# Rotary embedding on one core: the order of the loads and stores behind the fifth tile

## Chip, core and metric

The kernel runs on one NeuronCore of a Trainium2 chip. The metric is the device time of one launch in microseconds (us). Every time below is from six runs of the kernel before, or from one profiled execution of it.

## What is computed

The input x is a float32 array of 16 batches, 512 positions and 1024 numbers, 33.55 MB. The 1024 numbers are 16 heads of 64. In each head the first 32 numbers (x1) and the last 32 (x2) are turned against each other by the position's cosines and sines:

```python
x = x.reshape(batch, seq, num_heads, head_dim)
x1, x2 = (x[..., :half_dim].copy(), x[..., half_dim:].copy())
cos = cos[None, :, None, :].copy()
sin = sin[None, :, None, :].copy()
rotated = np.concatenate([x1 * cos - x2 * sin, x1 * sin + x2 * cos], axis=-1)
```

The output has the same size as x, so each number is read once, goes through a few operations, and is written once.

## The kernel before

**Tiles.** Two batches make a tile of 128 partitions: 64 partitions for each batch, and 8 positions (rows, k = 0 to 7) of 1024 numbers in every partition. That is 32 KB in a partition and 4.19 MB in a tile. There are NT = 8 tiles, numbered 0 to 7. Below, L3 is the load of tile 3 and S3 the store of tile 3.

**Buffers.** The pool `xp` has BUFS = 5 buffers of one tile each. The result is written over the input in the same buffer, and the store leaves from it. So tile 5 goes into the buffer of tile 0, tile 6 into that of tile 1, tile 7 into that of tile 2, and the load of tile n has to wait until the store of tile n - 5 has landed.

**Who does what.** For each row, GpSimd multiplies the swapped halves by the signed sines into a buffer `b` (line 155; seven rows of eight), VectorE multiplies the row by the cosines into a PSUM tile `ps` (line 156), and the two are added: by VectorE (line 145) for five rows, and for the rows 1, 4 and 6 by two TensorE matmuls with an identity (line 164), after which ScalarE copies the sum into the tile (line 167). In row 6 VectorE makes both products (lines 156 and 158). There are six buffers `b` and three of `ps`, so that GpSimd may run ahead of VectorE by some rows.

**The order of the transfers.** All DMAs are issued from one engine, SyncE (SP), in the order of the program: `load` is line 72, `store` line 76. The program runs under a manual schedule, so this order is the one written here. SP carries out one instruction after the other. Where a DMA has to wait, for its tile's last row or for a buffer to come free, all that is behind it on SP waits too.

Ahead of the loop stand tile 0 in four parts (lines 78 and 84), the two tables (lines 81 and 82) and the loads of tiles 1 to 4 (line 86). In the loop (lines 147 to 180), tile t is computed, then stored (line 173; the last tile in two halves, line 177), and behind the store of tile t, from t = 1 on, the load of tile t + 4 is issued (lines 179 and 180) as long as there is one. From the first store on, SP's order is therefore

```
S0 S1 L5 S2 L6 S3 L7 S4 S5 S6 S7(first half) S7(second half)
```

Of the kernel before, what the change touches and what calls it, by code (L numbers as in the profile page):

```python
# [13 lines left out]
BUFS = 5  # L14
# [12 lines left out]
def kernel(  # L27
# [21 lines left out]
    NT = batch // NB  # L49
# [18 lines left out]
    def load(t, lo=0, hi=KK):  # L68
        if tiles[t] is None:
            tiles[t] = xp.tile([P, F], FP32, name="xt")  # L70
        s = slice(lo * dim, hi * dim)
        nc.sync.dma_start(out=tiles[t][:, s], in_=x_v[t][:, s])  # L72

    def store(t, lo=0, hi=KK):
        s = slice(lo * dim, hi * dim)
        nc.sync.dma_start(out=out_v[t][:, s], in_=tiles[t][:, s])
# [36 lines left out]
    def cos_b(k):  # L113
        c = cos_t[:, k * half : (k + 1) * half]
        return bass.AP(tensor=c.tensor, offset=c.offset, ap=[c.ap[0], [0, 2 * nh], [1, half]])

    def over_heads(s):
        return bass.AP(tensor=s.tensor, offset=s.offset, ap=[s.ap[0], [0, nh], [1, hd]])

    def swapped(r, n):  # L120
        return bass.AP(
            tensor=r.tensor, offset=r.offset + half, ap=[r.ap[0], [hd, n], [-half, 2], [1, half]]
        )

    def swapped_signed(i):

        s = sns_t[:, i * hd : (i + 1) * hd]
        return bass.AP(
            tensor=s.tensor, offset=s.offset + half, ap=[s.ap[0], [0, nh], [-half, 2], [1, half]]
        )  # L130

    def pairs(r):
        return r.rearrange("p (a j) -> p a j", j=half)
# [4 lines left out]
    def halves(r):  # L138
        return r.rearrange("p (h a j) -> p h a j", a=2, j=half)
# [3 lines left out]
    def add():  # L143
        r, ps, b = pending.pop(0)
        nc.vector.tensor_tensor(out=r, in0=ps, in1=b, op=ALU.add)  # L145

    for t in range(NT):
        xt = tiles[t]
        for k in range(KK):
            r = xt[:, k * dim : (k + 1) * dim]  # L150
            ps = pr.tile([P, dim], FP32, name="ps")
            if k not in DVE_B:
                b = bp.tile([P, dim], FP32, name="b")
                sk = sns[:, k].rearrange("p a j -> p (a j)")
                nc.gpsimd.tensor_tensor(out=halves(b), in0=swapped(r, nh), in1=over_heads(sk), op=ALU.mult)  # L155
            nc.vector.tensor_tensor(out=pairs(ps), in0=pairs(r), in1=cos_b(k), op=ALU.mult)  # L156
            if k in DVE_B:
                nc.vector.tensor_tensor(  # L158
                    out=halves(r), in0=halves(r), in1=swapped_signed(DVE_B.index(k)), op=ALU.mult
                )  # L160
            if k in PE_ROWS:
                for c in range(0, dim, BANK):
                    rhs = swapped(r[:, c : c + BANK], BANK // hd) if k in DVE_B else b[:, c : c + BANK]
                    nc.tensor.matmul(  # L164
                        out=ps[:, c : c + BANK], lhsT=ident, rhs=rhs, start=False, stop=True, skip_group_check=True
                    )
                nc.scalar.copy(out=r, in_=ps)  # L167
            else:
                pending.append((r, ps, b))
            while len(pending) > (1 if k + 1 < KK else 0):  # L170
                add()
        if t < NT - 1:
            store(t)
        else:
            lo = 0
            for hi in LAST_OUT:
                store(t, lo, hi)
                lo = hi
        if t >= 1 and t + BUFS - 1 < NT:
            load(t + BUFS - 1)  # L180


# [33 lines left out]
```

## Time and profile before

| what | value |
|---|---|
| median of 6 runs | 164.62 us (164.43 to 165.4) |
| the profiled execution, its own time | 164.45 us |
| its span, first to last instruction | 162.5 us |
| VectorE busy | 132.3 us, 81% of the span |
| GpSimd busy | 130.2 us, 80% |
| TensorE matmuls busy | 82.7 us, 51% |
| ScalarE busy | 25.6 us, 16% |
| DMA packets | 3042, 67.26 MB, mean 414 GB/s |
| whole-tile loads, median from issue to landing | 29.7 us (7 of them) |
| whole-tile stores, median from issue to landing | 29.1 us (7 of them) |
| halves of the last store | 14.2 us (2 of them) |

The span is what the profiler saw between the first and the last instruction; the execution's own time has 1.95 us more around it. "Issue to landing" runs from the instruction on SP to the moment when the last of the 16 DMA engines has reported its share. It holds the transfer itself and the time that it stood in the queue behind earlier transfers. In the slices of the span (40 equal pieces of 4.06 us) a digit is a share in tenths, and 9 means 90% or more. In the views of SP a line such as `63.26 0.34 SPq L72` is an instruction that starts at 63.26 us and takes 0.34 us to issue. In the list of waits, the three numbers are the total in us, how many waits, and the longest.

### The profile page before, as it was taken

To read this page: it belongs to the slowest core of one execution; us is meant where nothing else is said; L and a number is where in the kernel's file an instruction comes from. 1 tells how busy PE (TensorE), PEld (TensorE's weight loads), DVE (VectorE), ACT (ScalarE), POOL (GpSimd) and SP (SyncE) were. 2 spreads that over 40 slices of the span, in tenths; PEclk is the share of its full clock that TensorE was granted. 3 is DMA by queue.
4 is the path that set the end of the run, shared out by engine and by line. 5 is a ranking of instruction groups with operands and counts; after the bars stand their busy time and mean duration, and the time that the engine had idled before them with its cause. 6 is when DMAs were issued, how large, how long until landed. Compare 5 with 4: busy or idle time off the path is not lost.

```text
span 162.5 us, 602 instructions
## 1 busy us (share of the span) xinstructions
PE 82.7 (51%) x106; PEld 25.7 (16%) x106; DVE 132.3 (81%) x118; ACT 25.6 (16%) x25; POOL 130.2 (80%) x62
## 2 busy tenths in 40 slices
PE   6207282644728362745663785289429833872000
PEld 1102021112202120211121212112102210220000
DVE  1197638999999999999999999999999999992000
ACT  0000511220220222022202210211220222022000
POOL 1099999999999999999999999999997999200000
PEclk9955555597895879695675558555955585557655
DMA  5999999998999999999999999999999999999991
GB/s 177 383 421 470 435 460 395 444 460 387 452 452 371 435 443 411 454 427 419 427 435 411 460 421 403 460 427 419 468 403 411 468 411 443 452 395 419 427 431 60
DMA packets 3042, 67.26 MB, mean 414 GB/s; under 512 B 352, under 2 KB 480, under 8 KB 480
## 3 DMA queue, kind: packets, MB, share of 16 engines
q1 hardware_dynamic: 3040, 67.24, 97.2%
q14 instruction: 2, 0.02, 0.0%
HBM read 33.69 MB, written 33.55 MB: 414 GB/s over the span
## 4 chain that ended last, share of the span: by engine, by line
DVE 55%; PE 12%; issue 10%; POOL 7%; ACT 4%; DMA 3%; SPq 0%; DVEq 0%; POOLq 0%
DVE ps L156 32%; DVE xt L145 17%; PE ps L164 12%; POOL b L155 7%; DVE xt L158 6%; ACT xt L167 4%; DMA b<-in_sin_dram 3%; PE tab L104 0%; PE tab L105 0%; DVE sns L107 0%; SPq L72 0%; DVE sns L108 0%; DVEq L156 0%; POOLq L155 0%
## 5 line engine op out<-in xcount | busy, mean ns | idle before, releaser
L155 POOL TENSOR_TENSOR b<-xt,sns 128x1024 f32<-128x1024 f32 x56 | 129.5, 2346 | 8.2 <-DVE sns L108 7.1
L156 DVE TENSOR_TENSOR ps<-xt,tab 128x1024 f32<-128x1024 f32 x64 | 76.7, 1226 | 6.8 <-ACT xt L167 5.8
L164 PE MATMUL ps<-b,ident 128*128 128x512 f32 x64 | 52.5, 968 | 49.2 <-DVE ps L156 40.5
L145 DVE TENSOR_TENSOR xt<-ps,b 128x1024 f32<-128x1024 f32 x40 | 48.1, 1218 | 0.9 <-POOL b L155 0.9
L167 ACT COPY xt<-ps 128x1024 f32<-128x1024 f32 x24 | 24.3, 1012 | 105.9 <-PE ps L164 95.0
L164 PE MATMUL ps<-xt,ident 128*128 128x512 f32 x32 | 26.4, 972 | 11.8 <-DVE xt L158 8.1
L164 PEld LDWEIGHTS ps<-b,ident 128*128 128x128 f32 x64 | 15.9, 273 | 83.1 <-issue 43.7
L164 PEld LDWEIGHTS ps<-xt,ident 128*128 128x128 f32 x32 | 8.4, 290 | 31.3 <-DVE xt L158 18.9
L158 DVE TENSOR_TENSOR xt<-xt,tab 128x1024 f32<-128x1024 f32 x8 | 9.8, 1221 | 0.3
L107 DVE TENSOR_SCALAR sns<-tab 128x256 f32<-128x256 f32 x1 | 0.4, 425 | 5.9 <-PE tab L105 5.9
L167 ACT ACT_TABLE_LOAD x1 | 1.3, 1283 | 16.9 <-PE ps L164 16.9
L95 PE MATMUL ps<-zero 128*128 128x512 bf16 x6 | 2.7, 627 | 1.2 <-DVE zero L89 1.2
L104 PE MATMUL tab<-b,spread 64*128 64x256 f32 x2 | 0.7, 414 | 2.5 <-DMA b<-in_sin_dram 2.5
L95 PEld LDWEIGHTS <-zero 128*128 128x128 bf16 x6 | 0.7, 135 | 2.3 <-DVE zero L89 1.2
L89 DVE MEMSET zero<- 128x256 uint32 x1 | 0.3, 272 | 0.9 <-PEq L197 0.9
L104 PEld LDWEIGHTS tab<-b,spread 64*128 64x128 f32 x2 | 0.3, 184 | 3.4 <-issue 3.4
L105 PE MATMUL tab<-b,spread 64*128 64x256 f32 x2 | 0.6, 376 | 0.0
L103 DVE COPY spread<-ident 64x64 f32<-64x64 f32 x2 | 0.3, 184 | 0.2 <-POOL ident masks.py:199 0.2
masks.py:197 POOL MEMSET ident<- 128x128 f32 x1 | 0.2, 204 | 0.3 <-POOLq L197 0.3
L108 DVE COPY sns<-tab 128x256 f32<-128x256 f32 x1 | 0.4, 415 | 0.0
L105 PEld LDWEIGHTS tab<-b,spread 64*128 64x128 f32 x2 | 0.4, 184 | 0.1
masks.py:199 POOL TENSOR_SCALAR_AFFINE_SELECT ident<-ident 128x128 f32<-128x128 f32 x1 | 0.3, 292 | 0.1
(5 smaller groups left out, 0.6 us busy)
## 6 DMA issues: line engine op xcount, KB each, us to landing
xt<-in_x_dram SPq DMA_DIRECT2D x7, 4096.0 KB, 29.7
out_dram<-xt SPq DMA_DIRECT2D x7, 4096.0 KB, 29.1
xt<-in_x_dram SPq DMA_DIRECT2D x4, 1024.0 KB, 7.6
out_dram<-xt SPq DMA_DIRECT2D x2, 2048.0 KB, 14.2
b<-in_sin_dram SPq DMA_DIRECT2D x1, 64.0 KB, 5.1
b<-in_cos_dram SPq DMA_DIRECT2D x1, 64.0 KB, 4.9
```

The costliest lines, as they stand in the source:

```text
L89: nc.vector.memset(zero, 0.0)
L95: nc.tensor.matmul(out=ps[:, c : c + BANK], lhsT=zero[:, :P], rhs=zero, start=True, stop=True)
L104: nc.tensor.matmul(out=sin_t, lhsT=spread, rhs=sin_sb, start=True, stop=True)
L105: nc.tensor.matmul(out=cos_t, lhsT=spread, rhs=cos_sb, start=True, stop=True)
L107: nc.vector.tensor_scalar_mul(out=sns[:, :, 0, :], in0=sin_k, scalar1=-1.0)
L108: nc.vector.tensor_copy(out=sns[:, :, 1, :], in_=sin_k)
L145: nc.vector.tensor_tensor(out=r, in0=ps, in1=b, op=ALU.add)
L155: nc.gpsimd.tensor_tensor(out=halves(b), in0=swapped(r, nh), in1=over_heads(sk), op=ALU.mult)
L156: nc.vector.tensor_tensor(out=pairs(ps), in0=pairs(r), in1=cos_b(k), op=ALU.mult)
L158: nc.vector.tensor_tensor(out=halves(r), in0=halves(r), in1=swapped_signed(DVE_B.index(k)), op=ALU.mult)
L164: nc.tensor.matmul(out=ps[:, c : c + BANK], lhsT=ident, rhs=rhs, start=False, stop=True, skip_group_check=True)
L167: nc.scalar.copy(out=r, in_=ps)
```

## The change

In the loop the rule for the later loads is replaced. Loads 5, 6 and 7 are now all issued in one place, behind the store of tile NT - BUFS - 1 = 2, in place of one behind each of the stores of tiles 1, 2 and 3.

```diff
@@ -176,8 +176,9 @@
             for hi in LAST_OUT:
                 store(t, lo, hi)
                 lo = hi
-        if t >= 1 and t + BUFS - 1 < NT:
-            load(t + BUFS - 1)
+        if t + 1 == NT - BUFS:
+            for n in range(BUFS, NT):
+                load(n)
```

From the first store on, SP's order becomes

```
S0 S1 S2 L5 L6 L7 S3 S4 S5 S6 S7(first half) S7(second half)
```

Nothing else differs: the instructions of the four compute engines, their order, the sizes of the transfers and the buffers are the same. Each of the three loads still waits for the store that was in its buffer (S0, S1 and S2).

## The prediction

> **What bounds the kernel now.** I read the slices of the span first, with the DMA queues below them.
>
> ```profile
> POOL 1099999999999999999999999999997999200000
> ...
> DMA  5999999998999999999999999999999999999991
> ...
> q1 hardware_dynamic: 3040, 67.24, 97.2%
> ...
> HBM read 33.69 MB, written 33.55 MB: 414 GB/s over the span
> ```
>
> The DMA row stands at nine tenths or more from the second slice to the last but one, and goes on when GpSimd and every other engine are empty. One queue, q1, holds all transfers and fills 97.2% of the 16 engines' span. The chain of waits says something else: it follows compute (VectorE 55% of it), down to the copy on ScalarE at 147.42 us that releases the last store. That chain leaves out the queue. The last store's own view tells it:
>
> ```profile
> L76 SPq DMA_DIRECT2D out_dram<-xt x1: 333/333/333, 148.5 to 148.5; - x1
> ...
> DMA to landing us min/median/max: 12.9/12.9/12.9
> ```
>
> This half store of 2 MB is issued at 148.5 and lands 12.9 us later. By the trace's landing records the store ahead of it lands at 156.53 and it lands at 161.37, so 4.84 us is its own time and about 8 us is standing in line. Compute could end 8 us later and nothing would change. The bound is the line of transfers.
>
> Now the line itself. Each transfer lands 16 times, once for each DMA engine; the last of the 16 counts. Calling load and store of tile n Ln and Sn, those records give: L1 23.73, L2 33.44, L3 43.15, L4 53.49, S0 63.18, S1 72.88, L5 83.13, S2 92.82, L6 102.97, S3 112.72, L7 122.61, S4 132.30, S5 141.97, S6 151.67, and S7 in two halves 156.53 and 161.37. (The issue plus the time to landing gives the same to 0.1 us: 148.5 + 12.9 = 161.4.) The steps between them:
>
> - load behind load: 9.71, 9.71
> - store behind store: 9.70, 9.67, 9.70; two halves 4.86 and 4.84
> - store behind load: S0 9.69, S2 9.69, S3 9.75, S4 9.69
> - a load that a store follows: L4 10.34, L5 10.25, L6 10.15, L7 9.89
>
> So a load with a store behind it ends late, by 0.63, 0.54, 0.44 and 0.18 us over 9.71. The packet records say where in the load: a 32 KB packet takes 1.213 us nearly everywhere, but from 79.6 to 81.3 us, at the end of L5, some fifteen take 1.24 to 1.56 us, likewise at 97.0 to 101.2 (L6), 118.7 to 120.4 (L7) and, longest, up to 1.94 us, at 49.3 to 51.5 (L4). The starts of L5, L6 and L7, where a load follows a store, show none to speak of. The turn from load to store costs; the turn back does not. The first engine to land loses nothing over these rounds (S1 71.98 to S4 129.76 us, 57.8 for six transfers), but the last sets the end, and the gap between first and last grows from 0.9 us at S1 to 2.5 at S4 and stays there to the end.
>
> **The change, part by part.** The same 20 DMAs of the same sizes go out and no compute instruction moves on its engine; only SP's order differs. Before, behind S1: L5 S2 L6 S3 L7 S4 S5 S6 S7. After: S2 L5 L6 L7 S3 S4 S5 S6 S7. Loads with a store behind them: four before (L4, L5, L6, L7), two after (L4, L7).
>
> *The line.* L4, S0 and S1 are as before: S1 at 72.88. Behind it: S2 9.69, L5 and L6 at 9.71 each, L7 at 9.71 plus one turn, S3 to S6 at 9.69 each, S7 9.70. Without the turn: 72.88 + 9.69 + 29.13 + 38.76 + 9.70 = 160.16. One turn is the unknown. Rows of the same kind give 0.18 (L7), 0.44 (L6), 0.54 (L5) and 0.63 (L4). They fall as the engines drift apart (first to last 0.9 us ahead of L5, 1.65 ahead of L6, 2.2 ahead of L7), so they look like the price of all engines turning together. In the new order the spread ahead of L7 should still be S1's 0.9, hence I take L5's 0.54: the last store lands at 160.70 against 161.37, **0.67 us earlier**. The ends: a turn at nothing saves 1.21; one that costs as much as the three it replaces (1.16) saves 0.05, the 0.05 being S3's slow step.
>
> *Does the line stay full?* SP's timeline of before:
>
> ```profile
> 47.20 0.34 SPq L76 DMA_DIRECT2D out_dram<-xt  x1
> 63.26 0.34 SPq L72 DMA_DIRECT2D xt<-in_x_dram  x1
> 63.70 0.90 SPq L76 DMA_DIRECT2D out_dram<-xt  x1
> 72.96 0.34 SPq L72 DMA_DIRECT2D xt<-in_x_dram  x1
> 81.12 0.33 SPq L76 DMA_DIRECT2D out_dram<-xt  x1
> 92.89 0.34 SPq L72 DMA_DIRECT2D xt<-in_x_dram  x1
> ```
>
> and from the queue's waits (total, number, longest):
>
> ```profile
> SPq L72 <- DMA out_dram<-xt: 35.3, 3, 15.6
> ```
>
> Issues take 0.34 us each, and three loads wait 35.3 us in all for the store that empties their buffer. SP stands still meanwhile, and the next store behind it too. New times: S2 waits for tile 2's last copy as it does now and is out by 64.6. L5 needs S0 landed (63.18), so it goes at about 64.7. L6 needs S1: 72.9. L7 needs S2, landing at 72.88 + 9.69 = 82.57. So SP waits some 8 and 9 us, two waits in place of three. Behind the L7 wait stands only S3, ready at 81.1, now issued at 83.0, 1.9 us later. The queue at each moment: S1 runs to 72.9 with S2 and L5 behind; S2 to 82.6 with L5 and L6; L5 to 92.3 with L6, L7, S3; S3's turn comes at about 112. No order is nearer than 8 us to being late. Cost nothing.
>
> *Does compute get its tiles in time?* L5 lands at about 92.3 instead of 83.1, 9.2 us later; L6 at 102.0, 1 us earlier; L7 at 112.2, 10.4 us earlier. GpSimd (line 155) is first at each tile; its starts by the trace are 89.24 (tile 5), 105.42, and for the last tile
>
> ```profile
> 122.77 16.23 POOL L155 TENSOR_TENSOR b<-xt,sns 128x1024 f32<-128x1024 f32 x7 [1.15 <-DMA xt<-in_x_dram]
> ```
>
> There it waits 1.15 us for L7. That wait goes, and one of about 3.1 us at tile 5 comes. With 16.2 us for a tile's seven products, tile 5 then ends on GpSimd at 108.5, tile 6 at 124.7, tile 7 at 140.9 (139.0 now). VectorE's start of tile 5 is at 96.69, 4.4 us after the landing; its first sum with a GpSimd product is at 100.23 (product ready at 94.6), its last at 112.40 (product 108.5). The tightest is row 4, TensorE's: its product is the fifth of tile 5, at 92.3 + 5 x 2.32 = 103.9, and the matmul waits for VectorE's 103.87 + 1.2 anyway. So VectorE keeps its times and S7's halves go out at 141.1 and 148.5, as now; they are needed at about 151.0 and 155.9. If this cover of 7 us were gone, the end would move by what is beyond it.
>
> **A rule against the change.** The row: alternating, a load and a store take 19.94, 19.90 and 19.58 us together, against 19.4 for two transfers in a run. The Trainium skill, in "DMA: Bandwidth & Descriptors", section "Where 436 GB/s comes from", puts the limit at the SBUF ports, 435.2 GB/s, with no term for direction or order. By it the queue's 67.24 MB take 154.5 us (an estimate from that page) in any order, and this change is worth 0. Runs of one direction agree with it (4.19 MB in 9.69 us is 433 GB/s); the alternating pairs don't. I follow the rows: 0.67 us.
>
> **The sum.** The profiled execution took 164.45 us (span 162.5, and 1.95 around it that stays). 164.45 - 0.67 = 163.78. The median of the runs shown is 0.17 above that execution: 164.62 - 0.67 = 163.95. I forecast **163.9 us**, 0.4% less.
>
> **The rivals.**
> - *The cost isn't the number of turns* (no change). The engine that lags may do so for a reason of its own, or one turn of eager engines takes what three took. For it: the mean landing of the 16 engines over the three rounds moves only 0.1 us more than runs of one direction would; all loss is in the spread. Against it: the stretched packets lie at the turns only, and the loss at L5 alone is under half of the total. It saves 0.05: about 164.55.
> - *The late fifth tile* (slower). L5 queued behind S2 starves GpSimd, then VectorE. For it: the load is 9.2 us later and GpSimd, 80% busy, must wait. Against: the slacks above. It decides only from an L5 landing past 96.7 (VectorE held), and moves the end once VectorE is over 7 us late, a landing near 104; one turn's price more than worked out doesn't do it, L5 would have to be overtaken by a whole transfer (102.0) and more. If it landed behind both L6 and L7, at 112, the end would be 112 - 104 = 8 us later, but the queue keeps its order; with half of such a disturbance (108) it is 4 us, less the 0.7 saved: 167.9.
> - *The turn is dearer after a longer run of loads* (same, or just slower). L4, behind four loads, has the dearest turn, 0.63, and its packets reach 1.94 us. Put at twice L4's price, 1.26, the end lands at 161.42: 164.7.
>
> **How the numbers follow.** Turns counted as worked out: 0.70. Cost not in the number of turns: 0.15. Dearer turn: 0.10. Late tile: 0.05. A measurement here tells 0.3% (0.5 us) from no change, so *faster* needs a saving of 0.5 us. The likeliest case gives that in most of its range (a turn of 0 to 0.63 saves 1.21 to 0.58; run-to-run scatter takes some away): 0.60 of 0.70, the rest *same*. The second and third cases are *same* but for a few hundredths on either side. Faster 0.61, same 0.29, slower 0.10. The range: from 164.62 - 1.3 = 163.3 to 164.8, which takes in the second and third cases.
>
> **What would show it.** In the profile after: L5 and L6 stepping by 9.71, only L4 and L7 above 10; the last S7 landing near 160.7 with a spread of about 1.5 to 2 us over the engines; two SP waits of 8 and 9 us for stores; GpSimd waiting 3 us at tile 5 and not at tile 7; VectorE's times unmoved. It is wrong if L7's step is near 11, if the spread still ends at 2.5 us, if L5 or L6 steps over 9.8, or if S7's second half is issued later than 156.

## The result and the profile after

The changed kernel takes 163.56 us (median of 17 runs, 162.91 to 164.63). The kernel before, run beside it, takes 164.9 us. The ratio is 0.9926, with a 95% interval of 0.991 to 0.9941, so it is faster by 0.74%, about 1.2 us. The profiled execution took 163.98 us, with a span of 162.1 us. A second comparison gave 0.9952 (0.9932 to 0.9972), about 0.8 us. Neither interval takes in no change; the two estimates of the size are 1.2 and 0.8 us.

The page of the profile after, slices and DMA queues:

```profile
POOL 1059999999999999999999499999999999900000
...
DMA  5999999999999999999999999999999999999991
...
q1 hardware_dynamic: 3040, 67.24, 97.3%
...
HBM read 33.69 MB, written 33.55 MB: 415 GB/s over the span
```

The DMA row has no digit under nine between the first slice and the last (the row before has one 8, in its tenth slice, which the prediction's reading passed over), and the queue's share is 97.3% against 97.2%. The line of transfers is full in both kernels. The page's averages can't show where 1 us went. One thing is visible: GpSimd's row has a dip (4) in the middle. That is its wait for tile 5, in its timeline (start, busy time, instructions, idle time before them):

```profile
72.20 18.55 POOL L155 TENSOR_TENSOR b<-xt,sns 128x1024 f32<-128x1024 f32 x8
93.09 48.56 POOL L155 TENSOR_TENSOR b<-xt,sns 128x1024 f32<-128x1024 f32 x21 [2.35 <-DMA xt<-in_x_dram]
```

GpSimd waits 2.35 us for L5 and then runs 21 products, three tiles, without a gap. The wait for L7 at the last tile is gone.

SP's timeline after, and its list of waits:

```profile
65.46 18.16 SPq L72 DMA_DIRECT2D xt<-in_x_dram  x3
83.73 66.55 SPq L76 DMA_DIRECT2D out_dram<-xt  x6
```

```profile
SPq L72 <- DMA out_dram<-xt: 16.6, 2, 9.3
```

The three loads go out between 65.46 and 83.62 us, and there are two waits for a store in place of three, 16.6 us in place of 35.3. Neither is where the time came from, since the line never ran dry.

The time is in the steps of the line itself. SP's views give them roughly, as issue plus time to landing. Before, for S1 and then L5, which has a store behind it:

```profile
L76 SPq DMA_DIRECT2D out_dram<-xt x1: 343/343/343, 47.2 to 47.2; - x1
DMA to landing us min/median/max: 25.7/25.7/25.7
...
L72 SPq DMA_DIRECT2D xt<-in_x_dram x1: 340/340/340, 63.3 to 63.3; - x1
DMA to landing us min/median/max: 19.9/19.9/19.9
```

After, for S2 and then L5, which has a load behind it:

```profile
L76 SPq DMA_DIRECT2D out_dram<-xt x1: 333/333/333, 65.0 to 65.0; - x1
DMA to landing us min/median/max: 18.2/18.2/18.2
...
L72 SPq DMA_DIRECT2D xt<-in_x_dram x1: 794/794/794, 65.5 to 65.5; - x1
DMA to landing us min/median/max: 27.5/27.5/27.5
```

Before, L5 lands at 83.2, 10.3 us behind S1 (72.9); after, at 93.0, 9.8 us behind S2 (83.2), each to 0.1 or 0.2 us. The landing records are finer. These are the steps of the last of the 16 engines from one transfer's landing to the next, taken from the landing records of three profiled executions of each kernel (the second and third come from the runs below):

```
before        L4 10.34  S0 9.69  S1 9.70  L5 10.25  S2 9.68  L6 10.15  S3 9.75  L7  9.89  S4 9.69
before, 2nd   L4 10.17  S0 9.75  S1 9.68  L5 10.05  S2 9.67  L6 10.31  S3 9.70  L7 10.32  S4 9.69
before, 3rd   L4 10.59  S0 9.75  S1 9.68  L5 10.12  S2 9.67  L6 10.11  S3 9.74  L7 10.14  S4 9.67
after         L4 10.26  S0 9.71  S1 9.69  S2  9.66  L5 9.71  L6  9.72  L7 9.81  S3  9.67  S4 9.68
after, 2nd    L4 10.15  S0 9.75  S1 9.83  S2  9.66  L5 9.70  L6  9.71  L7 9.72  S3  9.71  S4 9.66
after, 3rd    L4 10.24  S0 9.74  S1 9.70  S2  9.68  L5 9.67  L6  9.71  L7 9.84  S3  9.67  S4 9.69
```

Before, all of L5, L6 and L7 are long, together 1.16, 1.55 and 1.24 us over three times 9.71. After, they are 0.11, 0.00 and 0.09 over. From the last landing of L1, the first whole tile, to the end of the last store the three profiles of before take 137.65, 137.85 and 137.99 us, those of after 136.43, 136.39 and 136.43.

### The profile page after: what moved, and what is told of

Same layout as the page of the kernel before. It is cut to its first block, busy times and chain, and to the rows that moved or that the text cites. A ratio compares the mean times of both kernels' runs of the same rounds, so it can differ in the third digit from the quotient of the medians.

```text
span 162.1 us, 602 instructions
## 1 busy us (share of the span) xinstructions
PE 83.6 (52%) x106; PEld 26.1 (16%) x106; DVE 132.3 (82%) x118; ACT 25.6 (16%) x25; POOL 130.1 (80%) x62
## 3 DMA queue, kind: packets, MB, share of 16 engines
q1 hardware_dynamic: 3040, 67.24, 97.3%
## 4 chain that ended last, share of the span: by engine, by line
DVE 52%; PE 15%; issue 11%; POOL 6%; ACT 4%; DMA 3%; SPq 0%; DVEq 0%; ACTq 0%; POOLq 0%
DVE ps L156 30%; DVE xt L145 16%; PE ps L164 14%; POOL b L155 6%; DVE xt L158 5%; ACT xt L167 4%; DMA b<-in_sin_dram 3%; PE tab L104 1%; PE tab L105 1%; DVE sns L107 0%; SPq L72 0%; DVE sns L108 0%; DVEq L156 0%; ACTq L167 0%; POOLq L155 0%
## 5 line engine op out<-in xcount | busy, mean ns | idle before, releaser
L104 PE MATMUL tab<-b,spread 64*128 64x256 f32 x2 | 1.2, 697 | 3.0 <-DMA b<-in_sin_dram 3.0
L104 PEld LDWEIGHTS tab<-b,spread 64*128 64x128 f32 x2 | 0.5, 310 | 3.9 <-issue 3.9
L105 PE MATMUL tab<-b,spread 64*128 64x256 f32 x2 | 1.1, 631 | 0.0
L105 PEld LDWEIGHTS tab<-b,spread 64*128 64x128 f32 x2 | 0.7, 334 | 0.2
```

Source lines behind the costliest of these rows:

```text
L104: nc.tensor.matmul(out=sin_t, lhsT=spread, rhs=sin_sb, start=True, stop=True)
L105: nc.tensor.matmul(out=cos_t, lhsT=spread, rhs=cos_sb, start=True, stop=True)
```

## The experiments

A turn is a place in the queue where a store stands behind a load; a turn back is one where a load stands behind a store. In all of the experiments the profile is read in the same way: what the load's step at the last engine is over 9.71 us, the step of a load with a load behind it, is called the price of the turn. "Before" and "after" stand for the two kernels. Ratios are to the kernel before, run beside it on the same chip; the groups of experiments ran on several chips.

**The two kernels again.** No edit.

> The kernel before once more, for a second profile. Turn theory (each place where a store follows a load in the queue holds up the last DMA engine): the loads L5, L6 and L7 again step by more than 9.71 us at the last engine, by about 1.2 us in all, and the gap between first and last engine ends near 2.5 us. Rival (the lag was an accident of the one profiled execution): the excess over these three loads is under 0.5 us or lies in other transfers.

> A third profile of the kernel before, for the price of its turns at the last engine: by the first two, L5, L6 and L7 together are 1.0 to 1.6 us over three times 9.71.

Measured: ratio 1.0006 (0.9981 to 1.0031) for the second; the excess over L5 to L7 is 1.55 and 1.24 us. The lag isn't an accident of one execution.

> The changed kernel once more, for a second profile and its time. Turn theory: about 0.7% faster than before, and from the landing of S1 to that of the last store 87.2 to 87.5 us against 88.5. What it tells besides: whether the turn behind L7 is cheap (0.1 us as in the first profile) also when the engines come to it close together (first to last 0.9 us in place of 1.9). If the price depends on engines turning at the same time, a small gap ahead of L7 brings 0.4 to 0.6 us back; if it doesn't, 0.1 us again.

> A third profile of the changed kernel: L7, the only load with a store behind it besides L4, is 0 to 0.6 us over 9.71; L5 and L6 are within 0.05 us of it.

Measured: ratio 0.9952 (0.9932 to 0.9972). From S1's landing to the end the second profile takes 87.25 us. L7's price is 0.01 and 0.13 us. The gap between first and last engine ahead of L7 (at L6's landing) was 1.92, 1.17 and 1.44 us in the three profiles, its price 0.10, 0.01 and 0.13. Before, L5 turned at gaps of 0.90, 1.12 and 1.40 us and paid 0.54, 0.34 and 0.41. So how close together the engines turn doesn't set the price.

**More turns, with the same bytes: halves alternating against halves grouped.** Whole tiles are cut in two (a and b). Both kernels replace the order behind S1 by a list:

```diff
-        if t >= 1 and t + BUFS - 1 < NT:
-            load(t + BUFS - 1)
+ alternating: S2a L5a S2b L5b L6a | S3a L6b S3b L7a | S4a L7b S4b
+ grouped:     S2a S2b L5a L5b L6a L6b L7a L7b | S3a S3b | S4a S4b
```

(The lists are given in short, not as code; a bar marks where the next tile's computation stands.)

> Tiles 5 to 7 are loaded and 2 to 4 stored in halves of 2 MB, alternating: behind S1 five loads with a store behind them in place of one in the grouped halves. Turn theory at the mean price of the kernel before (1.16 us for three turns): 4 x 0.39 = 1.5 us slower than the grouped halves; if the price falls as the engines drift apart, 0.8 to 1.2 us slower, near the time of the kernel before. Rival (the lag comes from the compute engines' traffic to the on-chip memory at these times, not from the order): the same as the grouped halves within 0.3 us.

> The control for the alternating halves: the same halves in the changed kernel's order (S2, then L5 L6 L7, then S3 S4, each as two halves). Both theories: the time of the changed kernel within 0.4 us, since nothing but the number of DMAs differs.

Measured: alternating 1.0025 (1.0008 to 1.0042), grouped 0.9947 (0.9927 to 0.9967). With the same transfers and the same computing, the order alone makes 0.78%, 1.3 us. The DMA queues of the alternating halves:

```profile
q1 hardware_dynamic: 3904, 67.24, 97.3%
```

That is also the share of the first profile after, of a kernel faster by over 1 us, so one page's share doesn't tell the orders apart. (Over all profiles it moves a little: 97.0 to 97.2% before, 97.3 to 97.7% after, 97.8% for the grouped halves.) By the landing records, the alternating order's half loads with a store behind them took 5.31, 4.96, 5.68, 5.11 and 4.88 us, the grouped order's only one 4.97, against 4.90 for half loads in a run of the grouped order. The compute engines do the same work in both, so their traffic alone, without the order, doesn't make the lag.

**In between: two turns behind S1.** Two lists, `S1 L5 L6 | S2 | S3 L7 | S4` and `S1 L5 | S2 L6 L7 | S3 | S4`.

> Behind S1: L5 L6 S2 S3 L7 S4, so one turn behind a run of two loads (L6) and one behind a load between two stores (L7). Count theory (each turn costs about the same, 0.3 to 0.5 us): both steps long at the last engine, half of the gain left, about 0.35% faster than before. Enclosed theory (only a load with a store ahead of it and one behind pays): L6 within 0.1 us of 9.71, L7 0.2 to 0.6 us over it, 0.3 to 0.6% faster than before.

> Behind S1: L5 S2 L6 L7 S3 S4, the two kinds of turn in the other order and near the times where the kernel before had its first and the changed kernel its only one. Count theory: L5 and L7 both 0.3 to 0.5 us long. Enclosed theory: L5 0.3 to 0.6 us long, L7 within 0.1 us. A theory by time (turns around 110 us are cheap whatever stands ahead) expects the same as the enclosed one here, and a cheap L6 but a dear L7 in the other kernel only by accident; the two together tell them apart.

Measured: the first 0.9979 (0.9961 to 0.9997), the second 0.997 (0.9952 to 0.9988). Both lie between before and after, as a count of turns would have it, though the second's interval reaches that of after. The single prices do not: L6 0.17 and L7 0.76 in the first, L5 nothing and L7 0.61 in the second. For the second, SP's view of S1 and of L5, issue and time to landing:

```profile
L76 SPq DMA_DIRECT2D out_dram<-xt x1: 344/344/344, 49.3 to 49.3; - x1
DMA to landing us min/median/max: 23.8/23.8/23.8
...
L72 SPq DMA_DIRECT2D xt<-in_x_dram x1: 340/340/340, 63.4 to 63.4; - x1
DMA to landing us min/median/max: 19.3/19.3/19.3
```

S1 lands at 73.1 and L5 at 82.7, so L5 took 9.6 us by these rounded numbers (9.68 by the records), with S2 right behind it, where the kernel before took 10.3 in the same views. Up to this point the queue is that of the kernel before, transfer for transfer, where L5 paid 0.34 to 0.54 us in three profiles. So the same turn can be dear in one execution and free in another. The idea that only a load enclosed by stores pays doesn't hold: the enclosed L5 was free, and L7, with a load ahead of it, paid.

**The first turn moved.** L4 goes behind S0:

```diff
-    for t in range(1, BUFS):
+    for t in range(1, BUFS - 1):
         load(t)
...
+        if t == 0:
+            load(BUFS - 1)
         if t + 1 == NT - BUFS:
```

> The changed kernel with L4 issued behind S0 instead of behind L3: L3 S0 L4 S1 S2 L5 L6 L7 S3. One turn more. If the first turn of a launch is dear in itself (L4's 0.44 to 0.63 us in all profiles so far), L3 now pays it, 0.4 to 0.6 us, and L4, enclosed, pays 0.2 to 0.5 besides: slower than the changed kernel by 0.2 to 0.5 us. If L4 was dear for the time at which it turns or for its place, L3 is cheap and L4 pays about the same: the changed kernel's time within 0.2 us.

Measured: 0.9993 (0.9975 to 1.0011). By this ratio one turn more takes nearly all of the gain away; by the one profile, over a third of it (from L1's last landing to the end 136.94 us, against 136.4 after and 137.65 to 137.99 before). That it costs something, both show; how much, they don't. SP's timeline shows the new place of L4:

```profile
33.32 0.35 SPq L76 DMA_DIRECT2D out_dram<-xt  x1
33.72 0.42 SPq L72 DMA_DIRECT2D xt<-in_x_dram  x1
```

The price of the first turn went with it: L3 now pays 0.62 us (packets stretched at 39.8 to 41.9 us in place of 49 to 52), and L4, no longer first, pays 0.26. L7 paid 0.29 here. The first turn of the launch was dear in every profile with 128-partition loads only: 0.43 us at the least, 1.26 at the most. In all of them it also stands behind a long run of loads, so its being first and the length of the run aren't told apart.

**Half of the engines made late.** One load of 8 partitions ahead of L1 (the lines that give tiles 1 to 4 their buffers earlier are left out here):

```diff
...
+    nc.sync.dma_start(out=tiles[4][:8], in_=x_v[4][:8])
     for t in range(1, BUFS):
         load(t)
```

> The kernel before with one extra load of 8 partitions ahead of L1 (the part of tile 4 that L4 loads again), 32 KB on each of 8 of the 16 engines: these are 1.21 us late at every turn. It costs 1.2 us by itself at the last engine. If a turn is dear because engines make it at the same time (the prediction's view), L4 to L7 cost less at the last engine than their 1.2 to 1.8 us, and the time rises by less than 1.0 us. If engines that turn early hold up those still loading, the late half pays at each turn, and the time rises by 1.2 us or more.

Measured: 1.0212 (1.0187 to 1.0237), 3.5 us slower, for 256 KB. This doesn't tell what it was made for, because the small load held up all 16 engines and not eight by one packet: the 32 KB packets that started from 12.8 to 14.4 us took 3.3 to 4.5 us in place of 1.21. The slices of its page:

```profile
DMA  5999899999999999999999999999999999999991
GB/s 193 369 424 221 331 426 442 395 481 402 450 426 410 466 395 474 412 442 426 410 466 402 474 404 418 458 395 474 402 410 474 395 474 402 458 418 395 434 434 79
```

In the fourth and fifth slice (12 to 21 us) only 221 and 331 GB/s move although the engines are busy, and L1 lands at 26.55 to 28.09 us by engine in place of 23.08 to 23.73. That is 3.5 us at the first engine and 4.4 at the last; behind L1 the line was a little shorter than before, 137.10 us to the end. (L4 and L5 turned free here, L6 paid 0.23 and L7 0.56. S1, with a load behind it, stepped by 10.27 us at the last engine; one of the two instruction fetches told of below lies in it, and whether that is the reason wasn't tested.)

**The transfers alone.** The loop over k, that is every product, sum and matmul of the tiles, is left out of both kernels:

```diff
-        for k in range(KK):
-            r = xt[:, k * dim : (k + 1) * dim]
...
```

> The kernel before without its loop of products, sums and matmuls: the transfers alone, in the same order (the output is then the input). If the line of transfers is the whole bound, the time is that of the kernel before within 0.5 us. If the price of a turn comes from the compute engines' use of the on-chip memory beside it, L4 to L7 step by 9.71 us and it is 1 to 2 us faster.

> The changed kernel without its loop of products, sums and matmuls. Turn theory: 0.8 to 1.2 us faster than the transfers alone in the order of before. Rival (compute makes the price): the two are the same within 0.3 us.

Measured: 0.9974 (0.9957 to 0.999) in the order of before, 0.9918 (0.9898 to 0.9937) in the order of after. The page of the first:

```profile
DVE  1020000000000000000000000000000000000000
POOL 1000000000000000000000000000000000000000
DMA  5999989989989999999999999999999999999990
...
q1 hardware_dynamic: 3040, 67.24, 96.8%
```

VectorE and GpSimd are empty from the fourth slice on, and the DMA row stands at eight tenths or more all the same. All computing together costs 0.26%, 0.4 us. Between the two orders lies 0.56%, 0.9 us, without any computing beside it: L5 to L7 are 0.91 us over three times 9.71 in one, 0.01 in the other. (The two profiles are further apart, by 1.9 us in their spans, in part because the first turn, L4, which both orders have, paid 1.26 us in one and 0.83 in the other.) The price of a turn doesn't need the compute engines.

## Why the prediction was right, and where it was off

**The bound** was read rightly. The transfers alone take within 0.4 us what the kernel takes. The second half of the last store is issued at 149.9 us in the profile after and lands at 160.9:

```profile
L76 SPq DMA_DIRECT2D out_dram<-xt x1: 332/332/332, 149.9 to 149.9; - x1
DMA to landing us min/median/max: 11.0/11.0/11.0
```

It is 1.5 us later on SP than before (148.45 there) and lands 0.5 us earlier. Compute is not what ends the kernel.

**That turns cost** is shown by their number. Counting L4, four turns are before; three give 0.9979, 0.997 and 0.9993; two give 0.9926, 0.9952 and, in halves, 0.9947; six in halves give 1.0025. The lines of the profiles, from L1's last landing to the end, fall in the same order without an overlap (the kernel with the 8-partition load, where L1 itself was held up, left out):

| turns | us |
|---|---|
| 2 | 136.39 to 136.71 (5 profiles) |
| 3 | 136.94 to 137.46 (3) |
| 4 | 137.65 to 138.05 (4) |
| 6, of halves | 138.32 (1) |

**That the turn from load to store costs, and the turn back doesn't**, can't come from the number, since each order has one turn back fewer than turns. The steps show it: L4 has no turn back ahead of it and is long in every profile of the two kernels; L5 after has one ahead and no store behind, and stepped by 9.67 to 9.71.

**The sum** was 0.67 us; measured were 1.2 and, in the second comparison, 0.8. The term that was off is the price of the one turn that stays, L7's, "hence I take L5's 0.54". It measured 0.10, 0.01 and 0.13. Put into the sum, 0.1 gives 1.1 us saved, near its end "a turn at nothing saves 1.21". The forecast of 163.9 us is 0.3 above the median measured. That it came so near is in part luck: it started from 164.62 us for the kernel before, which took 164.9 in the comparison, and of the first comparison's saving of 1.2 us the sum misses 0.5.

**The reason for that price**, "they look like the price of all engines turning together", was wrong. In the prediction's one profile the price fell as the gap grew (0.54, 0.44, 0.18). In the second profile of before it rose along the same loads (0.34, 0.60, 0.61). In the third it stood still (0.41, 0.40, 0.43). The trend over three turns of one execution didn't hold. (One of the stretched packets that the prediction put down to L6's turn, at 97.0 us, ran beside an instruction fetch.) Over the three profiles the nine prices of L5 to L7 have a mean of 0.44 us, from 0.18 to 0.61; in the second profile's L7 the first engine's step is 9.54 us and the last's 10.32, so here the late end of the engines pays, and the gap widens.

**SP's waits** were given as about 8 and 9 us: they are two, 16.6 us in all, the longer 9.3. **GpSimd's wait** at tile 5 was given as 3.1 us; it is 2.35. **VectorE** kept its pace: its first product of tile 5 starts at 98.19 us, 1.5 later than before, but its first of tile 0 starts 1.5 later too (10.07 against 8.60), so the whole of its work is shifted and nothing is lost at tile 5.

**The rivals.** That the cost isn't in the turns is ruled out by the halves and by the transfers alone. The late fifth tile cost GpSimd its 2.35 us and held up neither VectorE nor the end. That a turn is dearer after a longer run of loads fails at L7 after, which stands behind two other loads and is the cheapest turn of its kernel (0.01 to 0.13); for a longer run it isn't settled, since L4 is the first turn too, and when L4 was moved, L3 was both again.

**The rule** of the Trainium skill that was weighed, "DMA: Bandwidth & Descriptors", section "Where 436 GB/s comes from", has no term for order. It holds within a run of one direction (4.19 MB in 9.68 us is 433 GB/s) and misses the turns, 0.44 us each in the mean of the nine before.

**What stays open**: why the turn behind a run of loads was free in all five profiles of the grouped orders (0.01 to 0.13 us) but not in three other kernels (0.17, 0.29 and 0.61), why an identical turn is free in one execution and costs 0.5 us in another, and why the first is dear (free only in the kernel with the 8-partition load). What goes on in a DMA engine at the turn wasn't seen.

## What to carry to other kernels

Where one queue of transfers is full from end to end, its busy share says little about what can still be gained: look at the steps between landings, at the last engine, and by what stands behind each transfer. Here a load with a store behind it, in the middle of the line, cost 0.4 us in the mean of the kernel before, and in a single execution anything from nothing to 0.8, so sort the transfers into runs of one direction as far as buffers allow, and check that the tile that now comes late (9 us here) still has cover. And don't read a trend into three values of one profile; a second profile costs little.

## What the runs showed of the hardware that wasn't expected

- The last engine loses more than the mean one. From L1's landing to the end, the mean of the 16 landings takes 136.40 to 136.49 us in the three profiles before and 135.82 to 136.15 after, 0.4 us less; the last landing takes 1.4 us less. The prediction counted the mean from S1 and found 0.1 us, "all loss is in the spread"; but S1's mean landing was itself late there: 9.87 to 9.97 us behind S0's before, where a load stands behind it, 9.73 to 9.75 after, where a store does. A store's delay of this kind is given back: S2 and L5 after together take 19.34 to 19.36 us at the mean, no more than two transfers in a run (19.4). At the end of the three profiles of before the gap between first and last engine is 2.5 to 3.1 us, after 1.2 to 2.2 us.
- The kernel's own instructions are fetched over the same DMA engines: two packets of 8 KB on q14, in the profile of before at 66.6 and 96.7 us. The one 32 KB packet of q1 that is stretched beside each takes 1.67 and 1.43 us in place of 1.21. The transfers alone have no such fetch in that time, nor such packets.
- A load of 8 partitions (256 KB) in front of full ones made the kernel 3.5 us longer, where its bytes at the usual rate would take 0.6 us.
